# Loading the first four batches of x one by one, each ahead of its y, in a batched matrix product

## The chip, the cores and the metric

The kernel runs on one core of one Trainium2 chip. The metric is the device time of one execution in microseconds (us). The profile shows one execution; its span, from the first to the last instruction, is some 1.8 us shorter than the device time. The kernel before takes 136.27 us (median of 3 runs, 135.98 to 136.44).

## The reference

```python
batch, dim_i, dim_j, dim_k = 32, 256, 512, 384       # float32
def reference(x, y):                                 # x: b,i,j   y: b,j,k
    return np.einsum('bij,bjk->bik', x, y).astype(np.float32)
```

There are 32 independent products of 256x512 by 512x384. x (16.8 MB) and y (25.2 MB) are read once, out (12.6 MB) is written once.

## The kernel before

Everything goes through one queue of transfers, issued by SyncE. Four batches of x come in one load of 2 MB: each batch on 32 partitions, with eight consecutive rows, 16 KB in one piece, on each. Each y is a load of 0.79 MB with 6 KB per partition. TensorE transposes x (through the identity), VectorE and ScalarE evict it to float16, round y to float16, TensorE multiplies two batches at a time, and both engines collect the result for a store.

```python
    def load_x(q):                                   # four batches, 128 x 16 KB
        x_of[q] = x_pool.tile([P, R, J], F32, name="x_sb")
        keep(nc.sync.dma_start(out=x_of[q],
             in_=x[q * Q : (q + 1) * Q].rearrange("g (p r) j -> (g p) r j", r=R)))

    def load(u):                                     # y of two batches, and x in time
        if u == 0:
            load_x(0)
        if (u + 1) * G % Q == 0 and u + 1 < U:
            load_x((u + 1) * G // Q)
        y_of[u] = y_pool.tile([P, G, NJ, K], F32, name="y_sb")
        for g in range(G):
            keep(nc.sync.dma_start(out=y_of[u][:, g],
                 in_=y[u * G + g].rearrange("(q t) k -> q t k", q=P)))
    ...
    for s in range(U + 2):                           # cut: two loads before the loop
        if s + ahead < U:
            load(s + ahead)
        if s == 0:
            transpose(0, 0)
            transpose(0, 1)
        if s >= 2:
            collect(s - 2)
        if 1 <= s <= U:
            multiply(s - 1)
        if s < U:
            round_y(s)
        ...                                          # transposes of the next four batches
        if s >= 2:
            store(s - 2)
```

## Time and profile before

| | before |
|---|---|
| device time, median | 136.27 us |
| span of the profile | 134.3 us |
| busy: TensorE, ScalarE, VectorE | 66%, 48%, 42% |
| share of the span that packets of the 16 DMA engines took | 97.8% |
| bytes moved | 54.53 MB |

The row of DMA shares on the page shows how to read this kernel: full from the second slice to the last but one, while no row of an engine is. The prediction shows these lines. Two words are used below: a *packet* is one contiguous piece that one of the 16 DMA engines moves, and a transfer *lands* when its last packet has.

### The profile page before, as it was taken

The page shows a single profiled execution, that of the slowest core. Times are in us where ns is not written, and L with a number is a line of the kernel's source. Part 1 is how long each engine was busy: PE and PEld are TensorE (multiplying, and loading weights), DVE is VectorE, ACT ScalarE, POOL GpSimd, SP SyncE. Part 2 cuts the span into 40 slices and gives each one's busy share as a digit, 9 for nine tenths or more (in the row PEclk, how much of TensorE's full clock was granted, in tenths as well). Part 3 has the DMA queues.
Part 4 walks back from the last instruction along what each step waited for, and adds up shares of the span by engine and source line. Part 5 has one row for each costly group of instructions (what it writes and reads, how often), then busy time and mean ns, then how long its engine had stood idle before and what let it go on. Part 6 is the DMA issues. An engine that isn't in the chain of part 4 may idle for free.

```text
span 134.3 us, 1968 instructions
## 1 busy us (share of the span) xinstructions
PE 88.5 (66%) x768; PEld 73.2 (55%) x768; DVE 56.2 (42%) x128; ACT 63.9 (48%) x129; POOL 0.7 (1%) x6
## 2 busy tenths in 40 slices
PE   0049494979299767786099771976439986597920
PEld 0049474768177666666078661864427665476810
DVE  0004717471743365711634318460363425628620
ACT  3004837662762476712744428560475336738610
POOL 2000000000000000000000000000000000000000
PEclk9999999999959999999968999999965899779997
DMA  5999999999999999999999999999999999999993
GB/s 112 415 400 450 409 417 421 456 388 421 417 448 408 409 428 421 457 394 417 413 443 436 408 417 428 442 422 402 425 423 444 426 402 427 419 427 419 417 394 158
DMA packets 8073, 54.65 MB, mean 407 GB/s; under 512 B 896, under 2 KB 896, under 8 KB 7040
## 3 DMA queue, kind: packets, MB, share of 16 engines
q1 hardware_dynamic: 8064, 54.53, 97.8%
q8 instruction: 6, 0.10, 0.3%
q14 instruction: 3, 0.02, 0.0%
HBM read 41.94 MB, written 12.58 MB: 406 GB/s over the span
## 4 chain that ended last, share of the span: by engine, by line
DMA 78%; PE 13%; ACT 4%; DVE 0%; issue 0%
DMA y_sb<-in_y_dram 40%; DMA x_sb<-in_x_dram 38%; PE o_ps L130 9%; PE t_ps L99 3%; ACT xt_sb L107 2%; ACT y_r L116 1%; ACT o_sb L143 1%; DVE o_sb L145 0%
## 5 line engine op out<-in xcount | busy, mean ns | idle before, releaser
L130 PE MATMUL o_ps<-y_r,xt_sb 128*64 128x384 f16 x512 | 52.4, 364 | 28.5 <-ACT o_sb L143 20.8
L130 PEld LDWEIGHTS <-xt_sb 128*64 128x64 f16 x512 | 39.1, 121 | 38.8 <-issue 22.4
L116 ACT CAST y_r<-y_sb 128x384 f16<-128x384 f32 x64 | 29.5, 514 | 38.7 <-DMA y_sb<-in_y_dram 38.6
L99 PE MATMUL t_ps<-identity,x_sb 128*128 128x128 f32 x256 | 36.9, 301 | 11.4 <-DMA x_sb<-in_x_dram 11.4
L99 PEld LDWEIGHTS t_ps<-identity,x_sb 128*128 128x128 f32 x256 | 34.1, 211 | 16.0 <-issue 16.0
L118 DVE CAST y_r<-y_sb 128x384 f16<-128x384 f32 x64 | 20.0, 356 | 46.7 <-DMA y_sb<-in_y_dram 46.7
L107 ACT CAST xt_sb<-t_ps 128x512 f16<-128x512 f32 x32 | 22.4, 731 | 23.6 <-PE t_ps L99 23.6
L105 DVE CAST xt_sb<-t_ps 128x512 f16<-128x512 f32 x32 | 22.6, 728 | 24.1 <-PE t_ps L99 23.8
L145 DVE COPY o_sb<-o_ps 128x384 f32<-128x384 f32 x32 | 16.3, 544 | 2.1 <-PE o_ps L130 2.1
L143 ACT COPY o_sb<-o_ps 128x384 f32<-128x384 f32 x32 | 13.9, 492 | 1.3 <-PE o_ps L130 1.3
L107 ACT ACT_TABLE_LOAD x1 | 1.3, 1283 | 0.7 <-PEq L192 0.7
masks.py:199 POOL TENSOR_SCALAR_AFFINE_SELECT identity<-identity 128x128 f32<-128x128 f32 x1 | 0.3, 294 | 0.1
masks.py:197 POOL MEMSET identity<- 128x128 f32 x1 | 0.2, 206 | 0.3 <-POOLq L192 0.3
L192 POOL MEMSET const-bfloat16-1.0<- 128x1 bf16 x1 | 0.1, 102 | 0.0
L192 POOL MEMSET const-uint8-127<- 128x1 uint8 x1 | 0.1, 102 | 0.0
L192 POOL MEMSET const-float32-0.0<- 128x1 f32 x1 | 0.1, 99 | 0.2 <-issue 0.2
L192 POOL MEMSET const-float32-1.0<- 128x1 f32 x1 | 0.1, 99 | 0.0
## 6 DMA issues: line engine op xcount, KB each, us to landing
y_sb<-in_y_dram SPq DMA_DIRECT2D x32, 768.0 KB, 17.9
x_sb<-in_x_dram SPq DMA_DIRECT2D x8, 2048.0 KB, 20.8
out_dram<-o_sb SPq DMA_DIRECT2D x16, 768.0 KB, 17.8
```

The source lines that it names most:

```text
L99: nc.tensor.transpose(t_ps[:, f, h], x_sb[:, h * NE + e + f, t::NJ], identity)
L105: keep(nc.vector.tensor_copy(dst, t_ps))
L107: keep(nc.scalar.copy(dst, t_ps))
L116: keep(nc.scalar.copy(yr_of[u][:, g, t], y_sb[:, g, t]))
L118: keep(nc.vector.tensor_copy(yr_of[u][:, g, t], y_sb[:, g, t]))
L130: nc.tensor.matmul(o_ps[g * M : (g + 1) * M], xt_sb[:, t, e, a * PQ : (a + 1) * PQ].rearrange("c p h -> c (p h)"), y_r[:, g, t], start=(t ...
L143: keep(nc.scalar.copy(o_of[u][:, e], ps_of[u][e]))
L145: keep(nc.vector.tensor_copy(o_of[u][:, e], ps_of[u][e]))
L192: nc = _bacc.Bacc("TRN2", target_bir_lowering=False, num_devices=1)
```

## The change

The intent is to let TensorE start sooner: it stood still for 8.7 us, until four batches of x had landed. The first four batches are now loaded one by one, each over all 128 partitions (two rows, 4 KB, on each), just ahead of their y, and are transposed as they come.

```diff
+    def load_first_x(b):
+        if b == 0:
+            x_of[0] = x_pool.tile([P, R, J], F32, name="x_sb")
+        keep(nc.sync.dma_start(
+                out=x_of[0][:, b * R1 : (b + 1) * R1],
+                in_=x[b].rearrange("(p r) j -> p r j", r=R1)))

     def load(u):
-        if u == 0:
-            load_x(0)
-        if (u + 1) * G % Q == 0 and u + 1 < U:
+        if (u + 1) * G % Q == 0 and u + 1 < U and u * G >= Q:
             load_x((u + 1) * G // Q)
         y_of[u] = ...
         for g in range(G):
+            if u * G < Q:
+                load_first_x(u * G + g)
             keep(nc.sync.dma_start(...))             # y, unchanged
+        if (u + 1) * G == Q:
+            load_x(1)
 ...                                                 # cut: transpose_first(b), 8 transposes
 ...                                                 # and 4 evictions of 128x256 for one batch
         if s == 0:
-            transpose(0, 0)
-            transpose(0, 1)
+            for b in range(G):
+                transpose_first(b)
 ...
+        if s == 1:
+            for b in range(G, Q):
+                transpose_first(b)
```

More of the change, by code (lines that the diff above doesn't have):

```diff
@@ L44 @@
     U = B // G
+    R1 = I // P
     const_pool = ctx.enter_context(tc.tile_pool(name="const", bufs=1))
@@ L70, in load_x @@
         )
+    def load_first_x(b):
+        if b == 0:
+            x_of[0] = x_pool.tile([P, R, J], F32, name="x_sb")
+        keep(
+            nc.sync.dma_start(
+                out=x_of[0][:, b * R1 : (b + 1) * R1],
+                in_=x[b].rearrange("(p r) j -> p r j", r=R1),
+            )
+        )
     def load(u):
-        if u == 0:
-            load_x(0)
-        if (u + 1) * G % Q == 0 and u + 1 < U:
+        if (u + 1) * G % Q == 0 and u + 1 < U and u * G >= Q:
             load_x((u + 1) * G // Q)
@@ L85, in load, with transpose_first @@
             )
+        if (u + 1) * G == Q:
+            load_x(1)
+    def transpose_first(b):
+        x_sb = x_of[0]
+        if b == 0:
+            xt_of[0] = xt_pool.tile([P, NJ, NE, Q * PQ, H], MM_DT, name="xt_sb")
+        for t in range(0, NJ, 2):
+            t_ps = tpsum_pool.tile([P, 2, R1, P], F32, name="t_ps")
+            for f in range(2):
+                for r in range(R1):
+                    keep(
+                        nc.tensor.transpose(
+                            t_ps[:, f, r], x_sb[:, b * R1 + r, t + f :: NJ], identity
+                        )
+                    )
+            for f in range(2):
+                src = t_ps[:, f].rearrange("c r (m w) -> c w r m", w=NE // R1)
+                dst = xt_of[0][:, t + f, :, b * PQ : (b + 1) * PQ].rearrange(
+                    "c (w r) p h -> c w r (p h)", r=R1
+                )
+                if f == 0:
+                    keep(nc.vector.tensor_copy(dst, src))
+                else:
+                    keep(nc.scalar.copy(dst, src))
     def transpose(q, half):
```

## The prediction

> **What bounds the kernel now.** I read the page first (busy shares, slices, DMA queue), then the issues, the windows of the two ends, the timeline of the head and the waits, and last the records of single DMA packets.
>
> The page, with its row of slices for DMA, its row of rates, and the queue:
>
> ```profile
> PE 88.5 (66%) x768; PEld 73.2 (55%) x768; DVE 56.2 (42%) x128; ACT 63.9 (48%) x129; POOL 0.7 (1%) x6
> ...
> DMA  5999999999999999999999999999999999999993
> GB/s 112 415 400 450 409 417 421 456 388 421 417 448 408 409 428 421 457 394 417 413 443 436 408 417 428 442 422 402 425 423 444 426 402 427 419 427 419 417 394 158
> ...
> q1 hardware_dynamic: 8064, 54.53, 97.8%
> ```
>
> No compute engine is busy for more than 66% of the span, and the 16 DMA engines carry packets for 97.8% of it. Only the first and the last slice are not full. So the kernel is one uninterrupted stream of 54.53 MB, and its time is the stream plus what stands before its first byte and after its last one. The stream begins about 1.8 us into the span (first packet record) and ends about 132.9 us into it. The 131.1 us between them are already filled by 131.4 us of packet time per engine (97.8% of 134.3 us), the excess being overlapping packets.
>
> The chain of waits says the same and shows where the stream could be broken:
>
> ```profile
> DMA 78%; PE 13%; ACT 4%; DVE 0%; issue 0%
> ```
>
> The head, in the timeline of the first 25 us (start, duration, engine, line; in brackets the idle time and what ended it):
>
> ```profile
> 0.74 0.38 SPq L66 DMA_DIRECT2D x_sb<-in_x_dram  x1
> ...
> 8.72 6.00 PE L99 MATMUL t_ps<-identity,x_sb 128*128 128x128 f32 x32 [8.72 <-DMA x_sb<-in_x_dram]
> ...
> 15.91 0.32 PE L130 MATMUL o_ps<-y_r,xt_sb 128*64 128x384 f16 x1 [1.19 <-ACT y_r L116]
> ...
> 21.04 0.93 ACT L116 CAST y_r<-y_sb 128x384 f16<-128x384 f32 x2 [0.95 <-DMA y_sb<-in_y_dram]
> ...
> 23.56 1.65 PE L130 MATMUL o_ps<-y_r,xt_sb 128*64 128x384 f16 x18 [1.85 <-ACT o_sb L143]
> ...
> 23.92 0.35 SPq L150 DMA_DIRECT2D out_dram<-o_sb  x1
> ```
>
> This is what the change aims at: TensorE stands still for 8.7 us until 2 MB of x have landed, the first multiply is at 15.9 us and the first store at 23.9 us. But while TensorE waits the DMA engines do not. The windows of one microsecond (last two columns: DMA share, GB/s) show a stream that runs from the first packets, with a slow start, and that thins out only in the last few microseconds:
>
> ```profile
> 2.00:3.00 1.00, 0.00 (x0) 0.00 (x0) 0.00 (x0) 0.01 (x1) 0.00 (x0) 1.00 0.64 115
> 3.00:4.00 1.00, 0.00 (x0) 0.00 (x0) 0.00 (x0) 0.00 (x0) 0.00 (x0) 1.00 0.78 311
> 4.00:5.00 1.00, 0.00 (x0) 0.00 (x0) 0.00 (x0) 0.00 (x0) 0.00 (x0) 1.00 0.94 393
> ...
> 128.00:129.00 1.00, 0.41 (x6) 0.03 (x1) 0.56 (x1) 0.27 (x1) 0.00 (x0) 1.00 1.05 436
> 129.00:130.00 1.00, 0.00 (x0) 0.00 (x0) 0.00 (x0) 0.00 (x0) 0.00 (x0) 1.00 0.78 326
> ```
>
> **How much a perfect stream could give.** In the packet records a 16 KB packet of x takes 611 ns (median of 1024), a 6 KB packet of y or out 234 ns (median of 6144), and one of the 896 completion packets 9 ns. Per engine that is (1024 x 611 + 6144 x 234 + 896 x 9) / 16 = 129.5 us. Against 131.1 us the stream loses some 1.7 us in all: about 1 us in the first packets (the first 120 packets of x average 743 ns instead of 611: 120 x 132 / 16 = 1.0 us), the rest at the thin end. A change that moves no fewer bytes can gain 1.7 us (1.2%) at the very best. That alone all but rules out the 2% for faster.
>
> **What the Trainium skill says.** "DMA: Bandwidth & Descriptors", section "Where 436 GB/s comes from", puts the fabric's ceiling at 435.2 GB/s for 16 ports. The trace agrees: 54.53 MB in 131.1 us are 416 GB/s, and no slice holds much more than 450. The same page, section "Why small descriptors are slow (HBM only)", gives each packet a fixed overhead of some cycles. The trace agrees in kind: from the two sizes, (611 - 234) / (16384 - 6144) = 0.0368 ns per byte, which leaves 234 - 226 = 8 ns per packet. "Perfetto Trace Analysis", section "DMA Optimizations", says that splitting DMAs lets some work start sooner "If DMA engines are generally idle". Here they are not, so the advice's condition fails. "TensorE: Matmul & The Clock Gate", section "HAM oscillation — how this bites in real kernels", says that waits longer than a window of about 3.4 us slow the clock of the next burst. The trace shows stretches of 3.4 to 6.8 us at 0.5 of the clock, after pauses of TensorE; this bears on a rival below.
>
> **The change, part by part.**
> Loads. One 2 MB load of x becomes four of 0.5 MB, each over 128 partitions with 4 KB for each, and they alternate with y0 to y3; x of batches 4 to 7 moves from before y2 to after y3. In the order of the DMA queue as built, everything from y4 on stands as before: the first 2 x 2.10 + 4 x 0.786 = 7.34 MB are the same bytes in another order. So from y4 on every load should land as before, later only by what the new packets cost. That is 512 packets of 4 KB in place of 128 of 16 KB: one is 8 + 4096 x 0.0368 = 159 ns (estimate), so 32 x 159 - 8 x 611 = 5.09 - 4.89 = +0.20 us per engine. Three more transfers bring 3 completion packets of 9 ns per engine: +0.03 us. Sum: +0.2 us on the path.
> Issue. Eight transfers can be in flight before the ninth waits for the first. They were 8.65 MB and are now 5.24 MB, still 12.6 us of stream; the ninth (x of batches 4 to 7) waits only for the first 0.5 MB. An issue takes 0.33 to 0.51 us against 1.3 us of stream for the smallest transfer, so the queue does not run dry.
> Compute in the head. Adding the windows' rates, the stream has delivered 0.52 MB at 3.7 us and 2.62 MB at 9 us. The old x0 was delivered in full at 7.7 us by the same count and released TensorE at 8.6 us, 0.9 us later. So the first transposes start near 4.6 us instead of 8.7, and the first multiply near 11 us instead of 15.9: 4 to 5 us sooner.
> What becomes of these 4 to 5 us. On TensorE, transposes for batches 4 to 7 stand ahead of the second multiply, and on VectorE and ScalarE their evictions stand ahead of the first collect. These need x of batches 4 to 7, which now lands after 7.34 MB, that is at 20.0 + 0.9 = 20.9 us (before, y3 landed at 21.0 with the same bytes ahead of it). Transposing takes 2.2 us, the last eviction 0.7, so the first collect and the second multiply begin near 23.5 us and the first store is issued near 24 us: within 0.5 us of the 23.56 and 23.92 above. The lead has gone before the first store.
> Evictions. Eight casts of 128x512 (728 to 731 ns) become 16 of half the size, each between 365 and 730 ns: 0 to 2.9 us more per engine, in a head where both mostly wait. Nothing on the path. The 32 transposes stay 32.
> The tail has the same instructions in the same order, behind loads that land 0.2 us later. The sum is +0.2 us.
>
> **Rivals.**
> 1. The earlier start carries through to the end. For: 8.7 us of TensorE's idle time at the start is the longest single wait. Against: the later ones are also for DMA (46.7 us on VectorE and 38.6 us on ScalarE for y), so every lead is lost at the next landing. It would make 131 to 132 us; I give it 1 in 100.
> 2. The slow start of the stream changes. The first packets of 16 KB take 1.0 to 2.0 us each; packets of 4 KB, with y among them, might lose less, or more if the loss is per packet. Nothing in the profile tells which: -0.7 to +1.0 us.
> 3. The queue starves: a wait for a completion or for the first collect holds the issue longer than the stream has work. Against: 7.1 us is the longest such hold before the change, against 17.8 us from issue to landing. If it came, 1 to 3 us: 137.5 to 139.5.
> 4. The tail shifts with the clock: a half-speed stretch over the last 64 matmuls (5.4 us) would hold the last store back. A pause long enough precedes the burst at 115 us, not the last one, and three runs differ by only 0.46 us: +-0.4 us.
>
> **Range and chances.** 136.27 + 0.2 = 136.5 us. Rival 2 spreads this by -0.7 to +1.0, rival 4 by 0.4, repetition by 0.25: 135.7 to 137.4 for 8 in 10. Over 2% is 2.7 us: faster would need more than the 1.7 us that the stream loses at all (0.01); slower needs starvation (0.03). Within 2%: 0.96.
>
> **What would show it.** Right: first transposes near 4.6 us, first multiply near 11, first store still near 24; DMA share of the queue again 97 to 98%; 512 packets of 4 KB near 159 ns; y4 landing within 0.5 us of before. Wrong: a hole in the DMA row after the first slice (rival 3), a first store at 19 us and an earlier end (rival 1), or a stream that is shorter or longer by over 1 us in its first 10 us (rival 2).

## The result

| | before | changed |
|---|---|---|
| device time, median of 6 runs | 136.17 us | 136.88 us |
| all runs | 135.98 to 136.44 | 136.51 to 137.15 |
| ratio | | 1.005 (95%: 1.0027 to 1.0074) |
| span of the profile | 134.3 us | 134.6 us |
| first transposes, first multiply | 8.72, 15.91 us | 4.02, 10.70 us |
| first store issued | 23.92 us | 24.93 us |

A ratio is the mean time of one kernel's runs over that of the other's of the same rounds, so it is not quite the ratio of the medians. The change counts as the same at 2%, but it is clear of noise: 0.7 us slower.

The page of the changed kernel, with the lines that answer to those of before: busy shares, the row of DMA shares, the row of rates, and the queue.

```profile
PE 91.3 (68%) x768; PEld 73.3 (54%) x768; DVE 56.8 (42%) x132; ACT 64.2 (48%) x133; POOL 0.7 (1%) x6
...
DMA  4999999999999999999999999999999999999992
GB/s 162 410 417 420 450 405 440 435 388 425 334 449 405 422 422 431 441 412 412 425 444 436 398 423 422 456 417 401 422 425 452 405 416 422 427 422 425 414 391 113
...
q1 hardware_dynamic: 8496, 54.53, 97.6%
```

The stream is still full from end to end. Two figures in the row of rates differ from before: the first slice moved more (162 against 112 GB/s), and the eleventh, 33.7 to 37.0 us, only 334 (before 417).

The head in the timeline of the changed kernel (start, duration, engine, line; in brackets the idle time and what ended it):

```profile
4.02 1.95 PE L112 MATMUL t_ps<-identity,x_sb 128*128 128x128 f32 x8 [4.02 <-DMA x_sb<-in_x_dram]
...
10.70 0.48 PE L170 MATMUL o_ps<-y_r,xt_sb 128*64 128x384 f16 x1 [1.33 <-ACT y_r L156]
...
20.65 2.76 PE L139 MATMUL t_ps<-identity,x_sb 128*128 128x128 f32 x16 [2.50 <-DMA x_sb<-in_x_dram]
...
23.82 2.39 PE L170 MATMUL o_ps<-y_r,xt_sb 128*64 128x384 f16 x18 [0.41 <-DVE o_sb L185]
...
24.93 0.35 SPq L190 DMA_DIRECT2D out_dram<-o_sb  x1
```

TensorE starts 4.7 us sooner and multiplies 5.2 us sooner, then waits at 20.65 us for x of batches 4 to 7. The second multiply begins at 23.82 us (before 23.56): the lead of the compute is gone before the first store.

The windows show what the stream itself did (the last three columns are the granted clock, the DMA share and the GB/s). First the changed kernel, then the stretch of 34 to 37 us of the kernel before:

```profile
2.00:3.00 1.00, 0.00 (x0) 0.00 (x0) 0.00 (x0) 0.01 (x1) 0.00 (x0) 1.00 0.84 311
3.00:4.00 1.00, 0.00 (x0) 0.01 (x1) 0.00 (x0) 0.00 (x0) 0.00 (x0) 1.00 1.11 449
34.00:35.00 1.00, 1.00 (x11) 1.00 (x9) 1.00 (x3) 1.00 (x3) 0.00 (x0) 1.00 1.07 363
35.00:36.00 1.00, 0.23 (x2) 0.15 (x2) 1.00 (x3) 1.00 (x3) 0.00 (x0) 1.00 0.88 227
36.00:37.00 1.00, 0.61 (x8) 0.54 (x9) 1.00 (x4) 1.00 (x3) 0.00 (x0) 1.00 0.97 399
```

```profile
34.00:35.00 1.00, 0.26 (x3) 0.18 (x2) 0.60 (x3) 0.60 (x2) 0.00 (x0) 1.00 1.08 442
35.00:36.00 1.00, 0.00 (x0) 0.00 (x0) 1.00 (x3) 1.00 (x3) 0.00 (x0) 1.00 1.00 412
36.00:37.00 1.00, 0.07 (x2) 0.07 (x3) 1.00 (x3) 1.00 (x3) 0.00 (x0) 1.00 0.98 406
```

The changed kernel's stream starts quicker: 311 and 449 GB/s in the third and fourth microsecond, where before it had 115 and 311. And it drops to 227 GB/s at 35 to 36 us, with the DMA share still at 0.88: the engines are not out of work, their packets take longer. In the packet records some forty 6 KB packets between 33.8 and 36.7 us took over 260 ns (median 234), most of them 300 to 600, and one took 1433.

Two sums of the packet records measure these two places. The *start loss* is the time by which the packets of the first 1 MB exceed the median for their size, divided by 16 engines; the *later loss* is the same for the bytes between 12.5 and 14.5 MB. Before they are 0.99 and 0.07 us, in the changed kernel 0.31 and 0.60 us. So 0.7 us were won at the start and 0.5 us lost again, in a place that the change doesn't touch: around y9, the last load before the first store enters the stream.

### The profile page after: what moved, and what is told of

It reads as the page before. It is cut to its first block, busy times and chain, and to the rows that moved or that the text cites. A ratio compares the mean times of both kernels' runs of the same rounds, so it can differ in the third digit from the quotient of the medians.

```text
span 134.6 us, 1983 instructions
## 1 busy us (share of the span) xinstructions
PE 91.3 (68%) x768; PEld 73.3 (54%) x768; DVE 56.8 (42%) x132; ACT 64.2 (48%) x133; POOL 0.7 (1%) x6
## 4 chain that ended last, share of the span: by engine, by line
DMA 80%; PE 8%; SPq 3%; ACT 3%; issue 1%; DVE 1%; DVEq 0%
DMA x_sb<-in_x_dram 42%; DMA y_sb<-in_y_dram 37%; PE o_ps L170 5%; PE t_ps L139 3%; SPq L94 1%; SPq L79 1%; ACT xt_sb L147 1%; ACT o_sb L183 1%; DVE o_sb L185 1%; ACT y_r L156 1%; DVE y_r L158 0%; SPq L190 0%; DVEq L185 0%; SPq L68 0%
## 5 line engine op out<-in xcount | busy, mean ns | idle before, releaser
L170 PE MATMUL o_ps<-y_r,xt_sb 128*64 128x384 f16 x512 | 54.9, 375 | 28.3 <-ACT o_sb L183 19.0
L170 PEld LDWEIGHTS <-xt_sb 128*64 128x64 f16 x512 | 39.7, 125 | 40.7 <-issue 20.2
L139 PEld LDWEIGHTS t_ps<-identity,x_sb 128*128 128x128 f32 x224 | 28.4, 210 | 7.9 <-issue 6.7
L147 ACT CAST xt_sb<-t_ps 128x512 f16<-128x512 f32 x28 | 19.6, 730 | 15.2 <-PE t_ps L139 15.1
L145 DVE CAST xt_sb<-t_ps 128x512 f16<-128x512 f32 x28 | 19.8, 728 | 14.5 <-PE t_ps L139 14.5
L112 PEld LDWEIGHTS t_ps<-identity,x_sb 128*128 128x128 f32 x32 | 5.2, 215 | 6.1 <-issue 4.3
L123 DVE CAST xt_sb<-t_ps 128x256 f16<-128x256 f32 x8 | 3.4, 424 | 8.8 <-PE t_ps L112 8.6
L125 ACT CAST xt_sb<-t_ps 128x256 f16<-128x256 f32 x8 | 3.0, 372 | 7.7 <-DVE xt_sb L123 7.4
```

Of the source, the lines that this page charges most:

```text
L112: nc.tensor.transpose(t_ps[:, f, r], x_sb[:, b * R1 + r, t + f :: NJ], identity)
L123: keep(nc.vector.tensor_copy(dst, src))
L125: keep(nc.scalar.copy(dst, src))
L139: nc.tensor.transpose(t_ps[:, f, h], x_sb[:, h * NE + e + f, t::NJ], identity)
L145: keep(nc.vector.tensor_copy(dst, t_ps))
L147: keep(nc.scalar.copy(dst, t_ps))
```

## The experiments

Twelve kernels ran. They tell apart which part of the change brings the quicker start, the slow packets and the longer time. This table gathers what all of them showed; 12.5 and 14.5 MB are the times in the profile at which so much had been moved, and the last columns are landings of y9 and of the last y (31), read from the issues.

| run | ratio (95%) | start loss | 12.5 MB at | 14.5 MB at | later loss | y9 | last y | span |
|---|---|---|---|---|---|---|---|---|
| before, first profile | 1 | 0.99 | 32.55 | 37.31 | 0.07 | 38.10 | 124.12 | 134.3 |
| c_before | 1.0009 (0.9993 to 1.0024) | 0.84 | 32.48 | 37.28 | 0.09 | 38.27 | 124.18 | 134.2 |
| e_order | 0.9994 (0.9982 to 1.0006) | 0.89 | 32.45 | 37.27 | 0.11 | 38.11 | 124.20 | 134.2 |
| e_onedma | 1.0019 (1.0006 to 1.0031) | 0.75 | 32.59 | 37.40 | 0.10 | 38.49 | 124.19 | 134.3 |
| e_order4k | 1.0007 (0.9988 to 1.0026) | 0.72 | 32.57 | 37.41 | 0.09 | 38.49 | 124.31 | 134.3 |
| changed, first profile | 1.0050 (1.0027 to 1.0074) | 0.31 | 32.02 | 37.44 | 0.60 | 38.89 | 124.43 | 134.6 |
| c_after | 1.0064 (1.0046 to 1.0082) | 0.20 | 31.95 | 37.47 | 0.69 | 39.46 | 124.96 | 135.2 |
| e_latecompute | 1.0058 (1.0040 to 1.0076) | 0.25 | 31.99 | 37.50 | 0.68 | 39.58 | 125.05 | 135.3 |
| e_xfirst | 1.0053 (1.0031 to 1.0076) | 0.25 | 32.29 | 37.50 | 0.51 | 38.95 | 124.49 | 134.8 |
| e_yfirst | 1.0054 (1.0029 to 1.0079) | 0.23 | 32.00 | 37.63 | 0.92 | 39.16 | 124.70 | 134.7 |
| e_twoloads | 1.0037 (1.0018 to 1.0055) | 0.65 | 32.36 | 37.35 | 0.22 | 38.88 | 124.50 | 135.1 |
| e_ypairs | 1.0069 (1.0036 to 1.0102) | 0.44 | 32.34 | 37.26 | 0.23 | 39.04 | 124.60 | 135.4 |
| e_split16k | 1.0326 (1.0306 to 1.0346) | 1.22 | 36.67 | 41.48 | 0.09 | 42.51 | 128.28 | 138.7 |
| e_onemore | 1.0360 (1.0338 to 1.0383) | 0.25 | 37.49 | 42.24 | 0.07 | 43.15 | 129.16 | 139.4 |

### Controls, and one part of the change at a time

**c_before** and **c_after** are the two kernels again, unchanged.

> The kernel before, unchanged, as a control. All theories: ratio 1.000 within 0.002. In its second profile the first 2 MB of x packets should again lose about 0.9 us per engine against their median, and there should be no cluster of slow packets near 34 to 36 us; if such a cluster turns up here too, it is not the change's.

> The changed kernel, unchanged, as a control for the size of the effect: ratio 1.003 to 1.008. Its first profile gained 0.5 us by the landing of y4 (22.39 against 22.89) and then lost about 0.55 us per engine in slow packets at 34 to 36 us. Theory A, the stall is the change's and makes the time longer: the cluster is there again at the same place. Theory B, the stall was a chance event and the loss lies in the small packets and extra transfers: no cluster, y9 lands earlier than the 38.1 of before, and the time is still longer somewhere else.

Both held. The second profile of the kernel before has no cluster of slow packets, the second of the changed kernel has it in the same place (344 and 240 GB/s at 34 to 36 us, one packet of 1616 ns). So theory A, that the stall belongs to the change, stood.

**e_order** keeps the 2 MB load with 16 KB packets and only moves x of batches 4 to 7 behind y3.

```diff
-        if (u + 1) * G % Q == 0 and u + 1 < U:
+        if (u + 1) * G % Q == 0 and u + 1 < U and u * G >= Q:
             load_x((u + 1) * G // Q)
 ...
+        if (u + 1) * G == Q:
+            load_x(1)
```

> Only the order of the loads is changed: x of batches 0 to 3 stays one load of 2 MB with 16 KB packets, but x of batches 4 to 7 moves behind y3 as in the changed kernel. Theory order (x of batches 4 to 7 later, first collect and store later, longer holds of the queue): as slow as the changed kernel, ratio 1.003 to 1.008. Theory packets (the 512 packets of 4 KB and the three extra transfers cost it): ratio 1.000 within 0.002.

The ratio is 0.9994. The first store was issued at 25.18 us, even later than in the changed kernel, and it cost nothing. The order, the later collect and the later store are ruled out as the cause.

**e_onedma** keeps one load and the old order, but spreads it over all partitions, so that its packets are of 4 KB. The transposes must then be those of the changed kernel; they stand together, for all four batches (not shown in the cut).

```diff
-                in_=x[q * Q : (q + 1) * Q].rearrange("g (p r) j -> (g p) r j", r=R),
+                out=x_of[0].rearrange("p (g r) j -> p g r j", r=R1),      # q == 0 alone
+                in_=x[0:Q].rearrange("g (p r) j -> p g r j", r=R1),
 ...                                                     # cut: the transposes
```

> Only the packets are changed: x of batches 0 to 3 is one load of 2 MB in the old order, but spread over all partitions, so in 512 packets of 4 KB, with the transposes batch by batch. Theory packets: plus 0.2 us from 32 packets of 159 ns against 8 of 611 ns, ratio 1.001 to 1.003, less what a quicker start gives back. Theory order or extra transfers: nothing, ratio 1.000, or 0.996 if the start loses 0.6 us less as in the changed kernel.

The ratio is 1.0019, that is 0.0019 x 136 = 0.26 us, as the theory of packets had it, and the median packet of 4 KB took 159 ns. This is a part of the loss, and it comes without slow packets at y9. Its interval is wide (0.08 to 0.42 us), and e_order4k below, with the same packets, had 1.0007 (0.9988 to 1.0026). The start was hardly quicker (0.75 us lost): small packets alone don't make it quick.

### Is it the number of transfers?

After these runs I thought that y9 might stall because it is the sixteenth transfer. Four runs were made on that.

**e_split16k** cuts the first load into four like the change, but by 32 partitions, in 16 KB packets, with the old transposes.

```diff
+                out=x_of[0][b * PQ : (b + 1) * PQ],
+                in_=x[b].rearrange("(p r) j -> p r j", r=R),
```

> The four first batches of x are four loads, each alternating with its y as in the changed kernel, but each goes to 32 partitions as before, in 16 KB packets; the transposes are those of the kernel before. So there are 59 transfers and the changed order, but no 4 KB packets and no earlier compute. Theory count (the stall at y9 comes from its being the 16th transfer): y9 again lands 3 us or more after y8 and 0.5 us or more is lost per engine near 34 to 36 us, ratio 1.004 to 1.010. Theory packets or theory compute (the stall needs the 4 KB packets, or the earlier start of the compute): no stall, y9 1.9 us after y8, ratio 0.998 to 1.002.

**e_onemore** is the changed kernel with x of batches 4 to 7 in two loads of 64 partitions.

```diff
-            load_x(1)
+            for h in range(2):                          # out=x_of[1][h * P // 2 : (h + 1) * P // 2]
+                ...
```

> The changed kernel with x of batches 4 to 7 in two loads of 64 partitions: one transfer more, so y8 is now the 16th and y9 the 17th. Theory count, tied to the 16th transfer: the stall moves to y8, 1.9 us sooner, near 32 to 34 us. Theory of a place in time or in the data: it stays at y9. Either way ratio 1.004 to 1.008.

Both missed what all theories expected of the time: 140.54 and 141.12 us. I had not thought of what a transfer over fewer partitions costs. "SBUF — State Buffer", section "Door 1: The DMA port swizzle (why `[64,N]` ≈ `[32,N]`)", states it: partitions 0 to 31 and 0 to 63 both reach 8 of 16 ports, with half the bandwidth. The traces agree. In e_split16k the second load of x landed 2.44 us after y0: 0.524 MB / 2.44 us = 215 GB/s; in e_onemore the second half of x landed 4.95 us after the first: 1.049 MB / 4.95 us = 212 GB/s. The window of 15 to 20 us in e_onemore, which holds nearly nothing but these loads:

```profile
15.00:20.00 5.00, 3.31 (x28) 2.62 (x24) 1.96 (x6) 2.29 (x6) 0.00 (x0) 1.00 0.99 206
```

A DMA share of 0.99 at 206 GB/s: full engines at half speed. So these two runs don't test what they were made for by their time. By their packets they do say one thing: with 16 or 17 transfers ahead of the first store, but a stream that is 4 to 5 us behind, y9 shows no slow packets (later loss 0.09 and 0.07).

**e_ypairs** joins y0 with y1 and y2 with y3; **e_twoloads** joins the four loads of x to two. Each has 14 transfers ahead of the first store.

```diff
+            keep(nc.sync.dma_start(out=y_of[u],          # e_ypairs, u < 2
+                in_=y[u * G : (u + 1) * G].rearrange("g (q t) k -> q g t k", q=P)))
```

```diff
-                in_=x[b].rearrange("(p r) j -> p r j", r=R1),
+                in_=x[b : b + G].rearrange("g (p r) j -> p g r j", r=R1),   # e_twoloads
```

> The changed kernel with y0 and y1 in one load and y2 and y3 in one: 57 transfers, 14 ahead of the first store instead of 16, with the same small first load and the same 4 KB packets. Theory count: the stall leaves y9, which is now the 14th; if it is tied to the 16th transfer it moves to x of batches 12 to 15 or thereabouts, and if to the 16 being full before the first store, it is gone and the time falls to 135.5 to 135.9 us, ratio 0.996 to 0.999, since the quicker start is kept. Theory packets: the stall stays at y9, ratio 1.004 to 1.008.

> The changed kernel with its four small loads of x joined to two of 1 MB, each ahead of two loads of y: 57 transfers, 14 ahead of the first store, 4 KB packets kept. Theory count: no stall at y9, the start still about 0.3 us quicker by the landing of y4, ratio 0.996 to 1.000. Theory packets: stall at y9 and ratio 1.004 to 1.008.

Neither theory was met: some slow packets were left (0.23 and 0.22 us), fewer than in the changed kernel, and the times were no better (1.0069 and 1.0037). The count was no good theory. What the table suggested instead was that the later loss is large where the start loss is small.

In both profiles the tail added to it. In e_ypairs a stretch of half clock lay on a multiply that took 2.79 us in c_before. First c_before, then e_ypairs:

```profile
115.61 2.79 PE L130 MATMUL o_ps<-y_r,xt_sb 128*64 128x384 f16 x32 [3.61 <-ACT o_sb L143]
```

```profile
116.04 5.33 PE L177 MATMUL o_ps<-y_r,xt_sb 128*64 128x384 f16 x32 [3.66 <-ACT o_sb L190]
```

The mean granted clock from 114 to 122 us was 0.57 there against 1.00, and the last store was issued at 130.83 us instead of 129. The device times of e_ypairs spread from 136.18 to 138.01 us. Whether the clock does that in all of them isn't shown, since one run alone of each experiment has a profile.

### Is it the lead?

**e_latecompute** is the changed kernel without its early compute: the transposes of all four batches stand together ahead of the first multiply.

```diff
         if s == 0:
-            for b in range(G):
+            for b in range(Q):
                 transpose_first(b)
 ...
-        if s == 1:
-            for b in range(G, Q):
-                transpose_first(b)
```

> The changed kernel with all its loads, but the transposes of all four first batches stand together ahead of the first multiply, as in the kernel before: the early compute is taken away. Theory loads (what costs time is how the loads are cut and ordered): ratio 1.004 to 1.008 again, and the slow packets at y9 near 34 to 36 us again, 0.5 us or more per engine. Theory compute (the earlier compute brings it): ratio 0.996 to 1.001 and no slow packets there.

1.0058, with the slow packets (320 and 221 GB/s at 34 to 36 us). Taking the early compute away changed neither the time nor the slow packets; the loads bring them.

**e_xfirst** has the four small loads ahead of y0 and the old order from then on.

```diff
+        if u == 0:
+            for b in range(Q):
+                load_first_x(b)
-            if u * G < Q:
-                load_first_x(u * G + g)
 ...                                                     # cut: x of batches 4 to 7 back ahead of y2
```

> The changed kernel with its four small loads of x all ahead of y0 and the order of before from then on; early compute kept. Four small loads and 4 KB packets without the alternation and without the later x of batches 4 to 7. Theory alternation or order (needed for the stall): no slow packets at y9, ratio 0.997 to 1.002. Theory four small loads on all partitions (enough for the stall): slow packets at y9, ratio 1.004 to 1.008.

1.0053, with the slow packets: no alternation and no other order is needed.

**e_order4k** has the order and the 4 KB packets, but one transfer: it is e_onedma with the two edits of e_order.

> The order of the changed kernel and its 4 KB packets, but x of batches 0 to 3 in one transfer ahead of y0 and the transposes all together. Theory packets with order: slow packets at y9 and ratio 1.004 to 1.008. Theory of the cut into several transfers: none, and ratio 1.000 to 1.003, as the single load of 4 KB packets in the old order had (1.0019).

1.0007, no quick start, no slow packets.

**e_yfirst** is the kernel before with one thing changed: y0 is issued ahead of x.

```diff
-        if u == 0:
-            load_x(0)
 ...                                                     # after the load of y0
+            if u == 0 and g == 0:
+                load_x(0)
```

> The kernel before with one thing changed: y0 is issued ahead of the first 2 MB of x, so the stream starts with 6 KB packets instead of 16 KB ones. No 4 KB packets, no extra transfer, same compute. If the slow start comes from the large first packets, it should lose 0.3 to 0.6 us per engine in the first 3 us instead of 0.8 to 0.9, and y5 should land 0.3 us or more sooner. Theory lead (a stream that is ahead by some tenths of a us meets the slow packets at y9): they appear here too, and the ratio is 1.000 to 1.006. Otherwise the lead is kept to the end: 135.6 to 136.0 us, ratio 0.996 to 0.999.

This is the run that separates the quick start from the rest of the change. It has no 4 KB packets, no more transfers and none of the new compute. Its stream starts quickly (0.23 us lost, even less than the 0.3 to 0.6 expected), and it meets the slow packets, more of them than any other. Its windows:

```profile
2.00:3.00 1.00, 0.00 (x0) 0.00 (x0) 0.00 (x0) 0.01 (x1) 0.00 (x0) 1.00 0.80 283
3.00:4.00 1.00, 0.00 (x0) 0.00 (x0) 0.00 (x0) 0.00 (x0) 0.00 (x0) 1.00 1.07 444
34.00:35.00 1.00, 0.85 (x8) 0.76 (x7) 1.00 (x3) 1.00 (x3) 0.00 (x0) 1.00 1.15 338
35.00:36.00 1.00, 0.00 (x0) 0.00 (x0) 1.00 (x3) 1.00 (x3) 0.00 (x0) 1.00 0.98 209
```

And it is as slow as the changed kernel: 1.0054. So a quick start that was got in another way comes with the same slow packets and a loss of the same size. The loss isn't made up in quite the same way: the changed kernel also pays 0.24 us at its end for its three more transfers, which e_yfirst doesn't have (step 4 below).

## Why the prediction was right, and where its sum was short

**What bounds the kernel** was right: the stream is full before and after, and the change moved the time by 0.5%. **The compute's lead is lost before the first store** was right too: first transposes at 4.02 us (predicted 4.6), first multiply at 10.70 (11), the second multiply at 23.82 (23.5), the first store at 24.93 (24, so 0.9 us later than predicted), and e_order showed that even such a delay costs nothing. e_latecompute showed the same from the other side: taking the early compute away left the time as it was. Rival 1 never appeared.

**The small packets** were right in size: 159 ns each, and 0.26 us (95%: 0.08 to 0.42) by e_onedma against the +0.2 us of the sum. The evictions of half size took 424 and 372 ns, within their range, and the loads hid them: e_latecompute, which has them too, ran as the changed kernel.

**y4 landing within 0.5 us of before**: it landed at 22.39 against 22.89 us, just at that limit and on the sooner side.

**The step that was short is the sum, "+0.2 us"**: from y4 on every load was to land as before, later only by what the new packets cost, and the tail was to be the same. It measured +0.7 us. Neither half held. y4 landed 0.5 us sooner, y9 0.8 and 1.2 us later, the last y 0.3 and 0.8 us later, and the end after the last landing grew by 0.24 us, where the prediction had 0.03 us for the three more transfers. That 136.88 us still lies in the range of 135.7 to 137.4 us is in part luck: rival 2, the slow start, came out as a gain of 0.7 us, and costs that no rival names outweighed it. (A slip on the way: the first eight transfers before were 2 x 2.10 + 6 x 0.786 = 8.9 MB, not 8.65; nothing rests on it. And slices of 456 and 457 GB/s do stand above the ceiling of 435.2 that it quotes; it is the mean of 416 that bears the comparison.) The runs showed a gain that is more than paid back:

1. The start loses 0.20 to 0.44 us instead of 0.7 to 1.0 where the first transfer is small (0.52 or 0.79 MB) and goes to all partitions. At 12.5 MB the changed kernel is 32.55 - 32.02 = 0.53 us ahead.
2. Between 12.5 and 14.5 MB it falls back: at 14.5 MB it is 37.44 - 37.31 = 0.13 us behind. From there on the stream as a whole keeps up: at 52 MB it is 0.07 us behind (c_after against c_before 0.09). The other three kernels with a start loss below 0.3 us and no delay in between (e_latecompute, e_xfirst, e_yfirst) do the same; those that start slowly don't; the two in between have a smaller lead and a smaller loss.
3. What doesn't keep up is the slowest engine, and a transfer lands with it. Each transfer ends with sixteen completion packets (896 of them for 56 transfers), and the trace keeps the times at which these sixteen completions raised the transfer's semaphore, though not the number of the engine. At y8 the first fifteen were done by 34.82 us in the changed kernel, 0.5 us sooner than before (35.32); at y9 by 37.15, level with before (37.19). The sixteenth, already 0.9 us behind the others at y8 in both kernels (35.70 and 36.26), came at 38.89 us for y9 instead of 38.10. One packet there took 1433 ns; that it belongs to this engine is an inference. In c_after the completions of y9 are at 37.04 and 39.46 us, in c_before at 37.06 and 38.27, and one packet took 1616 ns. This lateness lives on: the last y lands 85.5 us after y9 in the changed kernel's profiles and 86.0 us in those of before, so of 0.8 and 1.2 us of lateness 0.3 and 0.8 remain (each against the profile of before that was taken in the same rounds). The last store lands 0.15 and 0.77 us later (133.58 and 134.15 us against 133.43 and 133.38), in c_after again by one completion: the other fifteen are there by 133.36 us (before 133.33).
4. The end itself is longer. From the last landing to the end of the span it is 0.83 us in both profiles of before and 1.07 us in both of the changed kernel. The instruction records show SyncE waiting there for the semaphores of the transfers, one wait after another, each some 0.06 us. Eight semaphores are used in turn. With 56 transfers the last store has the one that is waited for last; with 59 its semaphore belongs to the first wait, and four more waits follow. So 0.24 us of the loss are the price of three more transfers, whatever the stream does. The other kernels agree: 0.83 or 0.84 us with 56 transfers, 0.94 with 57 (e_twoloads, e_ypairs), 1.07 with 59 and 1.09 with 60. Together, 0.15 + 0.24 and 0.77 + 0.24 are the 0.4 and 1.0 us by which the spans of the two pairs of profiles differ.

The late landing is seen in the timeline too. In c_before the last y is rounded from 124.20 us on; in c_after VectorE waits for its last half until 124.98:

```profile
124.20 0.93 ACT L116 CAST y_r<-y_sb 128x384 f16<-128x384 f32 x2 [0.85 <-DMA y_sb<-in_y_dram]
...
125.35 2.79 PE L130 MATMUL o_ps<-y_r,xt_sb 128*64 128x384 f16 x32 [1.17 <-DVE o_sb L145]
```

```profile
116.40 4.43 PE L170 MATMUL o_ps<-y_r,xt_sb 128*64 128x384 f16 x32 [2.63 <-ACT o_sb L183]
...
123.83 5.39 PE L170 MATMUL o_ps<-y_r,xt_sb 128*64 128x384 f16 x64 [0.86 <-ACT xt_sb L147]
...
124.98 0.63 DVE L158 CAST y_r<-y_sb 128x384 f16<-128x384 f32 x2 [0.30 <-DMA y_sb<-in_y_dram]
```

But the compute doesn't set the end of c_after. Its TensorE was late for a reason of its own, a burst at half clock (4.43 us, against 2.79 in c_before), and the last store was issued at 129.88 us instead of 128.82; still fifteen completions of that store came as early as before. The sixteenth came 1.80 us after the last completion of the store ahead of it (132.35 us), and eight packets of 234 ns take 1.87 us: if both are of one engine, it had no gap that an earlier store could have filled.

**Rival 3**, starvation, did not occur: the DMA share stays near 1 and the engines had packets. The hole in the row of rates at 34 to 37 us looks like it at first; the share tells the two apart. **Rival 4**, the clock, held the last store back in the profiles of e_ypairs and e_twoloads (issued at 130.83 and 130.71 us). In the profiles of the two kernels themselves the half clock lay on that burst in the first one of before (4.47 us) and in c_after, and step 3 accounts for the ends without it. The pause of 3.4 us that the prediction names doesn't sort these bursts: TensorE stood still for 2.63 us ahead of the slow one in c_after, and for 3.61 us ahead of the one at full clock in c_before.

**What stays open.** The slow packets at 34 to 36 us come where the stream is ahead there, and e_yfirst shows it without the rest of the change; *why* they come is not shown. The packets belong to y9, the last 0.79 MB before the first store, and they are slow on nearly all engines at once for about a microsecond (the first fifteen completions all lose their lead), and nothing in the trace begins there that the kernel before doesn't have too (both issue two loads of y then, at 33.85 and 34.39 us); the compute of e_order at the same time is the same and its stream doesn't slow down. e_split16k and e_onemore, whose streams reach y9 5 us later, don't have them. Whether the first store, the address or the moment makes them was not tried. Nor is it known why one engine is behind the others already at y8, in the kernel before as well (0.94 and 1.22 us in its two profiles). Every profile has one 16 KB packet of 1.0 to 1.1 us in a queue of instruction loads shortly before (27 to 30 us; 34 and 36 us in the two kernels that run 4 to 5 us behind), but no run tests a link. None of the runs beat the kernel before by more than noise, so it stays.

## What to carry to other kernels

Where one queue of transfers is full from end to end, look for the gain in the bytes, the packets and the landings, not in the idle time of an engine at the start: 5 us of earlier multiplying were worth nothing here, because the next load was no sooner. A lead of half a microsecond in the stream is only worth something if it is still there at the last landing; read it at several byte marks before counting on it. Judge a disturbance of the stream by its slowest engine, since the landing waits for that one: the stream as a whole was level again at 14.5 MB, and y9 was still 0.8 to 1.2 us late. And look at what comes after the last landing: three more transfers made it 0.24 us longer.

## What the Trainium skill lacked or had wrong

- "DMA: Bandwidth & Descriptors" gives a first-byte latency but says nothing on how quickly a stream gets up to rate. Here the first 1 MB lost 0.72 to 0.99 us per engine when the first transfer was of 2 MB, with packets of 16 or of 4 KB, and 0.20 to 0.44 us when it was of 0.52 or 0.79 MB over all partitions.
- No page that I read describes what happened at 34 to 36 us, and no run explains it: a full stream of 6 KB packets (234 ns) that falls to between 209 and 240 GB/s for a microsecond, in kernels whose stream was 0.5 us ahead.
- "Perfetto Trace Analysis", section "DMA Optimizations", says that smaller chunks may let some transfers start sooner, and that the whole task may end sooner "If DMA engines are generally idle". It doesn't say what a split costs when they are full. Here small packets in one transfer cost little (e_onedma 1.0019; e_order4k 1.0007, within its noise), and the kernels that cut the first 2 MB over all partitions into two or four transfers lost 0.4 to 0.7% (1.0037 to 1.0069, e_onemore left out), 0.11 to 0.24 us of it after the last landing. A quick start without a cut lost as much (e_yfirst, 1.0054).
- "SBUF — State Buffer", the section on the port swizzle, was right and would have saved two runs: 215 GB/s over 32 partitions, 212 over 64.
